# Linear attentions: the state's products before the level matrix's products in each result tile

## The chip, the cores and the metric

The kernel runs on one core of one Trainium2 chip. The metric is the device time of one execution in microseconds (us), lower is better. The core has a matrix engine (PE, with its weight loads listed apart as PEld), a vector engine (DVE), a scalar engine (ACT), GpSimd (POOL) and a sync engine (SP) that issues transfers. Matrix products land in PSUM; DVE and ACT read them from there.

## The reference

Two transformer blocks over 1024 tokens of width 1024. The change lies in the first one, which mixes two gated linear attentions (4 heads with values of 128, and 4 heads with values of 64; keys of 64 in both) with a stick-breaking attention. A linear attention of the reference, cut to what matters:

```python
def step(state, inp):                       # over chunks of the sequence
    q_c, k_c, v_c, g_c = inp
    b_cum = jnp.cumsum(g_c, axis=2)
    decay = jnp.exp(jnp.where(causal, b_cum[:, :, :, None, :] - b_cum[:, :, None, :, :], -jnp.inf))
    scores = jnp.einsum('bhtd,bhsd,bhtsd->bhts', q_c, k_c, decay)
    o_c = (jnp.einsum('bhts,bhsv->bhtv', scores, v_c)
           + jnp.einsum('bhtd,bhdv->bhtv', q_c * jnp.exp(b_cum), state))
    state = (jnp.exp(b_last)[..., None] * state
             + jnp.einsum('bhsd,bhsv->bhdv', k_c * jnp.exp(b_last - b_cum), v_c))
    return state, o_c
```

So a result is the sum of two products: the chunk's own scores with the values, and the decayed queries with the state carried in from the earlier chunks.

## The kernel before

The kernel takes chunks of 128 tokens, eight of them (`NT`), and treats the eight heads as four items of two heads each. Items 0 and 1 have values of 128 columns (`dv` 128), items 2 and 3 of 64. For an item:

- `gla_start` and `gla_state` make the carried state `S`, chunk by chunk: PE (L594) multiplies decayed keys and values into one PSUM tile `po` of which there is only one buffer, DVE (L599) adds it onto the decayed state before. These steps of the next item stand between the products of the present one.
- seven levels (`gla_level_a` to `gla_level_d`) fill the score matrices. For each, DVE takes differences (L619, L621), ACT exponentiates (L622), POOL and DVE multiply with keys and queries (L641, L643), PE makes eight products of 128 rows by 128 columns (L654) into a two-bank PSUM tile `gla_pb`, and DVE copies the cells of the level into `ST` (L663). `ST` holds the transposed score matrices of the whole item, 16 of 128 by 128, and exists once. Before the levels, DVE resets it with the diagonal (L606).
- `gla_qe` makes `qe`, the queries times the decay (ACT L667, DVE L668).
- `gla_out_a` makes the results. For each two-bank tile `po` of results (two for `dv` 128, one for `dv` 64) it issues, chunk by chunk and head by head, the product with `ST` (L686, it contracts over 128 rows) and for every chunk but the first the product with `S` (L688, it contracts over 64 rows). That is 16 and 14 products for an item, in either width. ACT then copies the tile out (L690).

All of these products are in fp32; the profile has two records for one. `gla_pb` and the result tiles `go_pb` share two PSUM buffers (`ps2`), so a result tile takes the buffer of the level before the last once that has been read.

Beside these steps, `fill` puts chunks of the block's input projections on PE (`unit_f`, L515 to L517, 128 by 512 moving columns, and `unit_v`) to use its time while the levels wait for other engines. They are used up before item 3 ends. After item 3 come its norm (`gla_out_b`, `gla_out_c`), the gate and the output projection of the block (L1124 to L1126), and then block two.

All engines run their own queue in order. The order in each queue is made when the program is built: the framework takes the instructions with their dependencies and lets a model of the timeline choose what comes next on each engine, so that an instruction written elsewhere can move others.

Of the kernel before, what the change touches and what calls it, by code (L numbers as in the profile page):

```python
# [15 lines left out]
P = 128  # L16
T = 1024
D = 1024
NT = T // P
# [135 lines left out]
class K:  # L155
# [516 lines left out]
    def gla_out_a(self, g):  # L672

        nc = self.nc
        S, v, dv, q, b, sc = (g[n] for n in ("S", "v", "dv", "q", "b", "sc"))
        st3 = self.ST.rearrange("p (c t) -> p c t", t=P)
        self.ph = f"go{dv}"
        qe = g["qe"] if "qe" in g else self.gla_qe(g, self.t4(tag="tmp"))
        g["o"] = []
        for i in range(2 * dv // P):  # L680
            po = self.ps2()
            for c in range(NT):
                cs = slice(c * P, (c + 1) * P)
                for h in ((i,) if dv == P else range(2)):
                    d = po[:, cs] if dv == P else po[64 * h:64 * h + 64, cs]
                    nc.tensor.matmul(d, v[:, c, h * dv:(h + 1) * dv], st3[:, 2 * c + h], start=True, stop=(c == 0))  # L686
                    if c:
                        nc.tensor.matmul(d, S[64 * h:64 * h + 64, c], qe[64 * h:64 * h + 64, cs], start=False, stop=True)  # L688
            o = self.gt("mx")
            nc.scalar.copy(o, po)  # L690
            g["o"].append(o)
# [1462 lines left out]
```

## Time and profile before

| | us |
|---|---|
| median of 3 runs (2403.15 to 2412.2) | 2404.36 |
| the profiled execution | 2410.1 |
| its span in the trace | 2408.2 |
| PE busy in it | 2255.4 (94%) |
| DVE busy | 1413.2 (59%) |
| POOL busy | 1169.6 (49%) |
| ACT busy | 892.4 (37%) |

The four places where results of an item are made lie at about 401 to 413, 489 to 511, 581 to 591 and 634 to 652 us of the span. The engines' shares over the whole span say little on these places, so they are read from the stretches around them. "PEclk" in a table of stretches is the granted clock of PE as a share of 2.4 GHz; 0.5 is its other level, 1.2 GHz. In the list of instructions in order of time, "x4" counts records (two for one fp32 product), the second number is the time from the first start to the last end, and what stands in square brackets is the idle time before and what ended it.

### The profile page before, as it was taken

Reading aid. Unit: us, or ns where it says so; the run is one execution under the profiler, and the core shown is the slowest. Engines: PE = TensorE matmul, PEld = TensorE weight load, DVE = VectorE, ACT = ScalarE, POOL = GpSimd, SP = SyncE. Lnnn points to the kernel's source line nnn. Section 1 sums busy time; section 2 is a strip of 40 time slices with the busy share of each in tenths; the row PEclk is TensorE's granted clock in tenths of the full one; section 3 lists DMA queues with packets and bytes.
Section 4 is the critical chain, followed back from the end, with each engine's and each line's share of the span. In section 5 each row is a group of like instructions: output and inputs, shape, how many; then the busy total and the mean of one; then the engine's idle time right before and its main releaser. Section 6 shows DMA issues by size and latency. Waiting matters only on the chain.

```text
span 2408.2 us, 30577 instructions
## 1 busy us (share of the span) xinstructions
PE 2255.4 (94%) x11689; PEld 1880.8 (78%) x11689; DVE 1413.2 (59%) x1982; ACT 892.4 (37%) x1459; POOL 1169.6 (49%) x924
## 2 busy tenths in 40 slices
PE   4999899999698999978999998999999999999997
PEld 3788787877577888767888886888888888888886
DVE  8576765758567457999867776436333333333335
ACT  4456632443214244855376775113211111111111
POOL 4247683654456353444467888520433443344331
PEclk9999989879599999989999999999999999999999
DMA  6442332312332222434531522331111111111112
GB/s 256 122 145 88 116 102 81 119 44 84 124 136 88 75 69 76 174 118 117 157 92 50 138 86 78 131 140 53 45 50 47 53 44 44 53 53 53 44 44 81
DMA packets 125759, 220.95 MB, mean 92 GB/s; under 512 B 48658, under 2 KB 72866, under 8 KB 125218
## 3 DMA queue, kind: packets, MB, share of 16 engines
q1 hardware_dynamic: 125602, 218.89, 27.4%
q8 instruction: 94, 1.54, 0.3%
q14 instruction: 63, 0.52, 0.1%
HBM read 166.85 MB, written 52.01 MB: 91 GB/s over the span
## 4 chain that ended last, share of the span: by engine, by line
PE 51%; DVE 5%; ACT 2%; issue 2%; POOL 1%; DMA 0%; POOLq 0%; DVEq 0%; ACTq 0%; SPq 0%
PE up_pb L1981 5%; PE up_pb L1979 5%; PE up_pb L1980 5%; PE br_ps L1925 3%; PE dn_ps L2034 3%; PE dn_ps L2036 3%; PE dn_ps L2035 3%; PE F_ps L230 2%; PE F_ps L228 2%; PE F_ps L229 2%; DVE topk_r L1589 2%; PE dn_pb L1980 1%; PE dn_pb L1981 1%; PE dn_pb L1979 1%; PE op_ps L1126 1%
## 5 line engine op out<-in xcount | busy, mean ns | idle before, releaser
L2038 DVE TENSOR_TENSOR br_h<-br_h,dn_ps 128x512 f32<-128x512 f32 x176 | 119.6, 685 | 237.6 <-PE dn_ps L2036 237.3
L205 POOL TENSOR_SCALAR up_wh<-up_raw 128x1024 fp32r<-128x1024 f32 x41 | 43.5, 1061 | 272.8 <-PE up_pb L1980 133.8
L2017 DVE SCALAR_TENSOR_TENSOR ffn_ws<-up_pb,cols,ffn_ws 128x1023 f32<-128x1023 f32 x66 | 84.5, 1281 | 138.9 <-ACT ffn_ws L2015 138.1
L2015 ACT ACTIVATE ffn_ws<-up_pb,cols 128x1024 f32<-128x1024 f32 x33 | 40.0, 1212 | 235.0 <-PE up_pb L1981 235.0
L1590 ACT ACTIVATE topk_r<-topk_r 128x896 bf16<-128x896 bf16 (+2 forms) x96 | 90.3, 945 | 58.8 <-DVE topk_r L1589 58.8
L210 POOL TENSOR_TENSOR up_wl<-up_raw,up_wh 128x1024 fp32r<-128x1024 f32 x41 | 98.5, 2403 | 20.2 <-PE up_pb L1981 17.5
L1979 PE MATMUL up_pb<-br_h,up_wh 128*128 128x512 f32 x264 | 102.7, 389 | 0.0
L1980 PE MATMUL up_pb<-br_h,up_wh 128*128 128x512 f32 x264 | 102.7, 389 | 0.0
L1981 PE MATMUL up_pb<-br_h,up_wl 128*128 128x512 f32 x264 | 102.7, 389 | 0.0
L1979 PE MATMUL up_pb<-op_fh,up_wh 128*128 128x512 f32 x264 | 102.7, 389 | 0.0
L1980 PE MATMUL up_pb<-op_fl,up_wh 128*128 128x512 f32 x264 | 102.7, 389 | 0.0
L1981 PE MATMUL up_pb<-op_fh,up_wl 128*128 128x512 f32 x264 | 102.7, 389 | 0.0
L2022 ACT CAST up_g<-ffn_ws 128x1024 fp32r<-128x1024 f32 x22 | 23.1, 1050 | 176.0 <-PE dn_ps L2035 97.7
L2034 PE MATMUL dn_ps<-dn_wh,up_g 128*128 128x512 f32 x192 | 75.2, 392 | 1.3 <-DVE br_h L2038 1.3
L242 PE MATMUL v_ps<-sb_wh,init_hh 128*128 128x256 f32 x256 | 75.1, 294 | 0.7 <-ACT v_st L500 0.7
L244 PE MATMUL v_ps<-sb_wh,init_hl 128*128 128x256 f32 x256 | 75.3, 294 | 0.0
L243 PE MATMUL v_ps<-sb_wl,init_hh 128*128 128x256 f32 x256 | 74.4, 291 | 0.7 <-POOL sb_wl L210 0.7
L2035 PE MATMUL dn_ps<-dn_wl,up_g 128*128 128x512 f32 x192 | 74.7, 389 | 0.0
L2036 PE MATMUL dn_ps<-dn_wh,up_g 128*128 128x512 f32 x192 | 74.7, 389 | 0.0
L210 POOL TENSOR_TENSOR sb_wl<-sb_raw,sb_wh 128x1024 fp32r<-128x1024 f32 x15 | 39.7, 2651 | 60.3 <-ACT sb_wh L209 41.7
L2020 POOL TENSOR_TENSOR ffn_ws<-ffn_ws 128x1024 f32<-128x1024 f32 x22 | 52.7, 2395 | 32.7 <-DVE ffn_ws L2017 32.7
L654 PE MATMUL gla_pb<-QB,gla_X 128*128 128x128 f32 x448 | 62.2, 291 | 6.5 <-POOL gla_X L643 6.5
(766 smaller groups left out, 7659.7 us busy)
## 6 DMA issues: line engine op xcount, KB each, us to landing
up_raw<-in_wu SPq DMA_DIRECT2D x43, 512.0 KB, 3.3
dn_raw<-in_wu SPq DMA_DIRECT2D x21, 512.0 KB, 3.2
sb_sp<-F_st SPq DMA_DIRECT2D x34, 256.0 KB, 2.0
sb_raw<-in_wu SPq DMA_DIRECT2D x15, 512.0 KB, 3.9
init_X<-in_wada SPq DMA_DIRECT2D x13, 512.0 KB, 4.3
c_raw<-in_wu SPq DMA_DIRECT2D x13, 512.0 KB, 3.4
br_raw<-in_wu SPq DMA_DIRECT2D x12, 512.0 KB, 3.8
bq_raw<-in_wu SPq DMA_DIRECT2D x11, 512.0 KB, 3.5
```

The source lines that it names most:

```text
L210: (nc.gpsimd if pool else nc.vector).tensor_tensor(l, raw, h, op=OP.subtract)
L242: nc.tensor.matmul(po, hh[:, k, ts], wh[:, cs], start=(k == 0), stop=False)
L244: nc.tensor.matmul(po, hl[:, k, ts], wh[:, cs], start=False, stop=(k == KT - 1))
L1590: nc.scalar.activation(y, y, AF.Copy, accum_out=cnt[:, j:j + 1])
L1979: nc.tensor.matmul(o, wh[:, s], self.hh[h][:, kk], start=(kk == 0), stop=False)
L1980: nc.tensor.matmul(o, wh[:, s], self.hl[h][:, kk], start=False, stop=False)
L1981: nc.tensor.matmul(o, wl[:, s], self.hh[h][:, kk], start=False, stop=(kk == KT - 1))
L2017: nc.vector.scalar_tensor_tensor(u[:, d:], p[:, :T - d], tap(2 - d), u[:, d:], op0=OP.mult, op1=OP.add)
L2034: nc.tensor.matmul(po, hi[:, ts], wh[:, cs], start=(k == 0), stop=False)
L2035: nc.tensor.matmul(po, hi[:, ts], wl[:, cs], start=False, stop=False)
L2036: nc.tensor.matmul(po, lo[:, ts], wh[:, cs], start=False, stop=(k == 1))
L2038: nc.vector.tensor_tensor(x, x, po, op=OP.add)
```

## The change

In each result tile, all products with `S` come first, head by head and chunk 1 to 7, and then all products with `ST`, chunk 0 to 7. The first product that is written into each of the two PSUM banks of a tile (chunk 1 and chunk 4) carries the start flag, and all the others accumulate. The number of products, their sizes and their operands are as before.

```diff
             po = self.ps2()
-            for c in range(NT):
-                cs = slice(c * P, (c + 1) * P)
-                for h in ((i,) if dv == P else range(2)):
-                    d = po[:, cs] if dv == P else po[64 * h:64 * h + 64, cs]
-                    nc.tensor.matmul(d, v[:, c, h * dv:(h + 1) * dv], st3[:, 2 * c + h], start=True, stop=(c == 0))
-                    if c:
-                        nc.tensor.matmul(d, S[64 * h:64 * h + 64, c], qe[64 * h:64 * h + 64, cs], start=False, stop=True)
+            heads = (i,) if dv == P else range(2)
+            d = lambda c, h: po[:, c * P:(c + 1) * P] if dv == P else po[64 * h:64 * h + 64, c * P:(c + 1) * P]
+
+            for h in heads:
+                for c in range(1, NT):
+                    nc.tensor.matmul(d(c, h), S[64 * h:64 * h + 64, c], qe[64 * h:64 * h + 64, c * P:(c + 1) * P],
+                                     start=c in (1, 4), stop=False, skip_group_check=True)
+            for h in heads:
+                for c in range(NT):
+                    nc.tensor.matmul(d(c, h), v[:, c, h * dv:(h + 1) * dv], st3[:, 2 * c + h], start=False, stop=True,
+                                     skip_group_check=True)
```

In the lists below, L687 and L691 of the changed kernel are L688 and L686 of the one before (products with `S`, products with `ST`), and later lines are shifted by four.

PE's queue at the results of item 1 (`go_pb_3998` is the first result tile, `gs_S` the state, `gs_po` the next item's state step, `F_ps` a projection), before:

```order
L517 MATMUL F_ps_4057<-init_hh_90,gla_wl_3918 128x512
L686 MATMUL go_pb_3998<-ST,gla_w_3123 128x128 [waits DVE_49]
L686 MATMUL go_pb_3998<-ST,gla_w_3123 128x128
L594 MATMUL gs_po_3840<-go_w_3592,gs_tmp_3818 64x64 [waits DVE_49]
L594 MATMUL gs_po_3840<-go_w_3592,gs_tmp_3818 64x64
L688 MATMUL go_pb_3998<-go_tmp_3995,gs_S_3253 128x128
L686 MATMUL go_pb_3998<-ST,gla_w_3123 128x128
L688 MATMUL go_pb_3998<-go_tmp_3995,gs_S_3253 128x128
```

The same place in the changed kernel:

```order
L516 MATMUL F_ps_4057<-init_hl_92,gla_wh_3917 128x512
L687 MATMUL go_pb_3998<-go_tmp_3995,gs_S_3253 128x128 [waits DVE_49]
L687 MATMUL go_pb_3998<-go_tmp_3995,gs_S_3253 128x128 x4
L594 MATMUL gs_po_3840<-go_w_3592,gs_tmp_3818 64x64 [waits DVE_49]
L594 MATMUL gs_po_3840<-go_w_3592,gs_tmp_3818 64x64
L687 MATMUL go_pb_3998<-go_tmp_3995,gs_S_3253 128x128 x2
L691 MATMUL go_pb_3998<-ST,gla_w_3123 128x128 x8
L687 MATMUL go_pb_4016<-go_tmp_3995,gs_S_3253 128x128
L594 MATMUL gs_po_3844<-go_w_3592,gs_tmp_3818 64x64 [waits DVE_49]
L594 MATMUL gs_po_3844<-go_w_3592,gs_tmp_3818 64x64
L687 MATMUL go_pb_4016<-go_tmp_3995,gs_S_3253 128x128 x6
L691 MATMUL go_pb_4016<-ST,gla_w_3123 128x128 x5
```

The alternation of the two sizes is gone. The set also begins four projection products earlier in the queue: nine of `F_ps_4057` stood ahead of it, now five do, and the four others stand behind it. The next item's state step still splits the sets.

DVE's queue before that place (`go_tmp_3995` is `qe`, and L663 is the last copy into `ST`), before:

```order
L668 TENSOR_TENSOR go_tmp_3995<-go_tmp_3995,gla_qkb_3117 128x1024 [waits Activation_49]
L745 SCALAR_TENSOR_TENSOR F_tmp_3888<-mix_mx_3893,F_tmp_3888 128x1024 [waits DMAHW5_49,DVE_49]
L619 TENSOR_TENSOR gla_X_4047<-go_qkb_3590 128x32x16
L621 TENSOR_TENSOR gla_X_4047<-go_qkb_3590 128x32x16
L663 COPY_PREDICATED ST<-lv,gla_pb_3950 128x1024 [waits PE_49]
L641 TENSOR_TENSOR QB_483<-gla_X_3962,go_qkb_3587 64x8x64 [waits Activation_49]
L599 SCALAR_TENSOR_TENSOR gs_S_3831<-gs_S_3831,gs_c_3766,gs_po_3836 128x64 [waits PE_49]
```

And in the changed kernel:

```order
L749 SCALAR_TENSOR_TENSOR F_tmp_3888<-mix_mx_3893,F_tmp_3888 128x1024 [waits DMAHW5_49,DVE_49]
L619 TENSOR_TENSOR gla_X_4047<-go_qkb_3590 128x32x16
L621 TENSOR_TENSOR gla_X_4047<-go_qkb_3590 128x32x16
L668 TENSOR_TENSOR go_tmp_3995<-go_tmp_3995,gla_qkb_3117 128x1024 [waits Activation_49]
L663 COPY_PREDICATED ST<-lv,gla_pb_3950 128x1024 [waits PE_49]
L641 TENSOR_TENSOR QB_483<-gla_X_3962,go_qkb_3587 64x8x64
L599 SCALAR_TENSOR_TENSOR gs_S_3831<-gs_S_3831,gs_c_3766,gs_po_3836 128x64 [waits PE_49]
```

The step that makes `qe` has moved back by three and now stands right ahead of the last copy into `ST`.

PE's queue at the results of item 3, where no projection is left (`gla_pb_4785` is the last level, `go_qkb_4664` is `qe`), before:

```order
L654 MATMUL gla_pb_4785<-QB_483,gla_X_4768 128x128 x7
L686 MATMUL go_pb_4800<-ST,go_w_3592 64x128 [waits DVE_49]
L686 MATMUL go_pb_4800<-ST,go_w_3592 64x128 x2
L688 MATMUL go_pb_4800<-go_qkb_4664,gs_S_4377 64x128
L686 MATMUL go_pb_4800<-ST,go_w_3592 64x128
L688 MATMUL go_pb_4800<-go_qkb_4664,gs_S_4377 64x128
```

And in the changed kernel:

```order
L654 MATMUL gla_pb_4785<-QB_483,gla_X_4768 128x128 x7
L687 MATMUL go_pb_4800<-go_qkb_4664,gs_S_4377 64x128 [waits DVE_49]
L687 MATMUL go_pb_4800<-go_qkb_4664,gs_S_4377 64x128 x13
L691 MATMUL go_pb_4800<-ST,go_w_3592 64x128 [waits DVE_49]
L691 MATMUL go_pb_4800<-ST,go_w_3592 64x128 x15
L708 MATMUL go_pg_4833<-h_488,go_tmp_4836 128x2 [waits PE_49,Activation_49]
```

Here there are two waits for DVE where there was one: 14 products behind the first, 16 behind the second.

## Rows read from the trace of the kernel before

**Rows 1.** Stretches: busy us (instructions) by engine, PE clock, DMA share, GB/s.

```profile
400.00:413.50 13.50, 13.50 (x73) 9.65 (x72) 1.12 (x3) 3.12 (x5) 1.26 (x1) 1.00 0.06 21
413.50:489.00 75.50, 72.08 (x397) 61.81 (x397) 58.32 (x52) 32.16 (x36) 46.70 (x22) 0.91 0.34 119
489.00:511.00 22.00, 21.56 (x74) 15.22 (x75) 5.87 (x9) 3.92 (x5) 4.25 (x3) 0.55 0.03 13
511.00:580.00 69.00, 65.67 (x377) 56.34 (x377) 58.54 (x57) 29.65 (x35) 36.28 (x19) 0.92 0.23 84
580.00:592.00 12.00, 12.00 (x78) 7.00 (x77) 2.89 (x4) 2.58 (x4) 1.26 (x1) 1.00 0.06 22
592.00:634.00 42.00, 26.88 (x188) 24.35 (x187) 40.54 (x31) 16.82 (x25) 30.87 (x20) 0.76 0.34 120
634.00:652.00 18.00, 17.52 (x60) 8.45 (x60) 1.72 (x3) 0.00 (x0) 0.56 (x1) 0.50 0.00 0
```

**Rows 2.** Who waited, 310 to 665 us: us in total, times, longest.

```profile
DVE ST L606 <- PE go_pb L686: 7.6, 3, 3.8
```

**Rows 3.** Item 0, PE in order of time: start us, us, records (x).

```profile
400.63 0.60 PE L686 MATMUL go_pb<-ST,sb_w 128*128 128x128 f32 x4
401.17 0.49 PE L688 MATMUL go_pb<-go_tmp,gs_S 64*128 64x128 f32 x2
401.58 0.49 PE L686 MATMUL go_pb<-ST,sb_w 128*128 128x128 f32 x2
...
413.38 0.49 PE L654 MATMUL gla_pb<-QB,gla_X 128*128 128x128 f32 x2
413.80 0.44 PE L594 MATMUL gs_po<-gla_w,gs_tmp 128*64 128x128 f32 x4
414.17 1.83 PE L654 MATMUL gla_pb<-QB,gla_X 128*128 128x128 f32 x14
```

**Rows 4.** Item 1, PE in order of time.

```profile
489.12 0.71 PE L686 MATMUL go_pb<-ST,gla_w 128*128 128x128 f32 x4 [1.74 <-DVE ST L663]
490.15 0.34 PE L594 MATMUL gs_po<-go_w,gs_tmp 128*64 128x64 f32 x4 [0.32 <-DVE gs_S L599]
...
491.25 0.79 PE L688 MATMUL go_pb<-go_tmp,gs_S 64*128 64x128 f32 x2
491.97 0.79 PE L686 MATMUL go_pb<-ST,gla_w 128*128 128x128 f32 x2
...
510.58 1.65 PE L654 MATMUL gla_pb<-QB,gla_X 128*128 128x128 f32 x6
```

**Rows 5.** Item 1, DVE in order of time: the last copy into ST.

```profile
486.62 2.44 DVE L663 COPY_PREDICATED ST<-lv,gla_pb 128x1024 f32<-128x1024 uint8 x1
```

**Rows 6.** Item 2, PE in order of time.

```profile
580.72 0.65 PE L686 MATMUL go_pb<-ST,go_w 128*64 128x128 f32 x6
...
591.27 2.05 PE L654 MATMUL gla_pb<-QB,gla_X 128*128 128x128 f32 x16
593.08 0.48 PE L515 MATMUL F_ps<-init_hh,gs_wh 128*128 128x512 f32 x1
```

**Rows 7.** Item 3 and what follows, all engines in order of time.

```profile
614.92 6.38 DVE L739 SCALAR_TENSOR_TENSOR go_tmp<-go_tmp,mix_X 128x1024 f32<-128x1024 f32 x1
...
615.14 3.78 PE L654 MATMUL gla_pb<-QB,gla_X 128*128 128x128 f32 x16 [6.47 <-POOL gla_X L643]
...
627.19 2.44 DVE L663 COPY_PREDICATED ST<-lv,gla_pb 128x1024 f32<-128x1024 uint8 x1
...
631.97 2.46 DVE L663 COPY_PREDICATED ST<-lv,gla_pb 128x1024 f32<-128x1024 uint8 x1
...
634.48 1.12 PE L686 MATMUL go_pb<-ST,go_w 128*64 128x128 f32 x6 [5.55 <-DVE ST L663]
...
652.28 1.01 ACT L690 COPY go_mx<-go_pb 128x1024 f32<-128x1024 f32 x1 [19.06 <-PE go_pb L688]
...
663.00 1.22 PE L1124 MATMUL op_ps<-mix_wh,F_mh 128*128 128x512 f32 x2
```

## Prediction

> **What bounds the kernel now.** PE is busy for most of the span, but that says nothing about a place of 10 to 20 us, so I read the table of stretches first [rows 1]. At the results of items 0, 1 and 2 (13.5, 22 and 12 us) PE is busy throughout, while DVE has 1.12, 5.87 and 2.89 us of work: the other engines wait for these products. In the two long stretches between, PE is busy for 72.08 of 75.5 and 65.67 of 69 us, and DVE for 58.32 and 58.54. PE is the bound there too, with DVE 10 to 17 us behind. Between 592 and 634 us it turns round: DVE 40.54 of 42 us, PE 26.88. The last stretch, 634 to 652 us, holds PE's products for item 3 and next to nothing else.
>
> The list of who waited gives the link from one item to the next: DVE's reset of `ST` waits for the last product that reads it, 7.6 us over three items [rows 2]. So an earlier end of the products with `ST` starts the next item's levels earlier.
>
> Then PE's list in order of time, place by place. In item 0 products of the two sizes alternate and start 0.41 to 0.42 us apart [rows 3]; eight level products of one size take 593.08 - 591.27 = 1.81 us, 0.226 each [rows 6]. A change of size therefore costs about 0.19 us at 2.4 GHz. Check: the item's 30 products with 28 changes and two state steps of 0.37 us (414.17 - 413.80) make 30 x 0.226 + 28 x 0.19 + 0.74 = 12.8 us, and 413.38 - 400.63 = 12.75 us is what they took [rows 3]. That PSUM accumulation in place causes the gap is excluded by the same rows: the state step L594 between two level products adds to neither tile, and the pair from 413.38 to 414.17 costs 0.79 us, 0.56 more than one product. In item 1 the spacing becomes 491.97 - 491.25 = 0.72 us [rows 4], with the granted clock at 0.55 over the stretch [rows 1], that is 1.2 GHz for most of it; PE had stood idle for 1.74 and 0.32 us just before. Eight products of one size at that level span 3.78 us [rows 7], about 0.45 each, so a change costs about 0.27 there.
>
> **The change, part by part.** It adds and removes no product. It takes away most changes of size, lets the products with `S` start before `ST` is ready, and moves a few neighbours.
>
> *Item 0.* By the new order, seven with `S`, state step, eight with `ST`, four, state step, three, eight. A state step between products of one size costs 0.56 [rows 3], one between two sizes 0.37 and a change. Sum: 30 x 0.226 + 3 changes x 0.19 + 0.56 + 0.56 = 8.5 us, 4.3 less.
>
> *Item 1.* `qe` now ends right before the last copy into `ST`, so the first five products with `S` (1.1 us) lie beside that copy, 486.62 to 489.06 [rows 5]. Nothing is gained yet: the state step behind them waits for DVE's L599, which still follows the copy, and starts at 490.15 as before [rows 4]. Behind that wait stand the 25 other products and the next levels. From 490.15 at full clock: step 0.27, 25 x 0.226, 4 changes, two steps of 0.56 inside a size, together 7.8 us, and four projection products (about 0.9 us) that before stood ahead: 498.9 where the trace has 510.58, 11.7 less. At 1.2 GHz from 491.25 on, as in the trace, 21 to 22 products at 0.45, 3 changes at 0.27, steps of 0.8 and projections of 1.8 end at about 505.2, 5.4 less. I take 8.5, the middle, since the idle time that went ahead of the low clock is still there, while the products behind it are closer together. The Trainium skill ("TensorE: Matmul & The Clock Gate", Part 1) says that "the default state is throttled, and activity releases the throttle". By that rule the denser set would regain 2.4 GHz inside the place, and the term would lie towards 11.7; the trace has the low level through the sparse set and cannot show the dense one.
>
> *Item 2.* 591.27 - 580.72 = 10.55 us [rows 6] become 30 x 0.226 plus three changes and two steps, about 7.9: 2.6 less. The price of a change in this width, from the same rows, is (10.55 - 6.8 - 0.6) / 28 = 0.11.
>
> *Item 3.* The result tile takes the buffer that DVE's copy from 627.19 to 629.63 reads [rows 7]. After it the 14 products with `S` can run in PE's idle 5.55 us ahead of 634.48: 14 x 0.226 = 3.2 us, at the low clock 6.3. They end between 632.8 and 635.9. The 16 with `ST` still wait for the last copy (634.43) and take 3.6 to 7.2 us. ACT's copy, at 652.28 before, starts between 638.1 and 642; with the products with `S` not begun early it would be 634.5 + 30 x 0.45 = 648. So 4 to 14 less; I take 11.3, near the low clock that this stretch shows (0.50) for the second set. What is late next is the same chain as before, the norm and the gate, which leads to the output projection at 663.00 without PE work beside it, so all of this term shifts the rest.
>
> *The other moves* (a `qe` step on DVE, state steps, two gate steps and their loads near 610 us) I cost at nothing: the same instructions, beside PE's work in the first three stretches. Where that cover is gone, near 615 us, L739 took 6.38 us [rows 7]; its start may move by a few us in either direction. I keep +-5 us for it.
>
> *Price of a product with 64 rows behind another with 64 rows.* No row shows it. Nearest rows: 0.226 (128 rows behind 128) and 0.41 (64 behind 128). It cannot cost more than with a change ahead of it, nor much less than a product that streams the same 128 columns. I take 0.226, as the stream is the same and only the rows in use differ. A rule of the Trainium skill speaks against it: "TensorE: Matmul & The Clock Gate", Part 3, What overlaps and what doesn't, has weight loads run beside products only where the row group differs. By it each product with `S` would go on paying its load, and the whole gain would be the second rival's below. In rows 6 eight level products in the same rows run at 0.226 with a load each, against that rule; for 64 rows no run here shows it.
>
> *Sum.* Items 0 to 2: 4.3 + 8.5 + 2.6 = 15.4, of which I let 14 through, since DVE has less than 17 us in hand in the stretches behind them and the state step still comes one at a time. With item 3: 14 + 11.3 = 25 us. The profiled execution (2410.1, its span 2408.2 and 1.9 around it) would take 2385; it lies 5.7 above the median of 2404.36, from which the forecast is 2379.
>
> **The rivals.**
>
> *Only the tail gains.* If DVE and POOL set the pace of the levels, what items 0 to 2 give is waited away. For: DVE is at 77 and 85% in the long stretches. Against: PE at 95% in the same rows, and DVE's waits for it. Then item 3 alone, 11.3: 2393.
>
> *Products with 64 rows stay slow* (0.41 each, 0.72 at the low clock). Half the changes' price stays: about 2 + 4.5 + 1 in items 0 to 2, and in item 3 the first set lasts until 638 to 640 and the second until 645, 7 less. Together about 14: 2390.
>
> *The clock turns it slower.* PE is done sooner and then waits for DVE and POOL; each wait can bring the low clock, as before 491 us. Its place is the two long stretches, where the projections run: a product that takes 0.226 takes 0.45, so each us of PE time at 1.2 GHz costs half a us. Their clock is 0.91 and 0.92 [rows 1], some 12 to 14 and 11 us at the low level. To eat 25 us it would take 50 more of their 145 us, a mean clock near 0.75, and it decides beyond that; at 0.65 (77 us more, 38 lost) the kernel would be 13 us slower: 2417. Against: after the results PE has projections to do at once, and only 3.4 us idle in each stretch now.
>
> *It doesn't do what it says*: DVE's waits could be set by a later instruction so that the first set waits for the last copy after all. In items 0 and 2 that changes nothing, in item 3 it gives 648: a total of about 18, 2386, inside the forecast's range.
>
> **How the numbers follow.** The forecast 0.70, only the tail 0.13, slow products 0.10, the clock 0.04, more than 36 us gained 0.03. The forecast's own range: items 0 to 2 between 11 and 19, item 3 between 4 and 14, the moved steps +-5, added without all ends at once: 15 to 35 us, 2369 to 2389. The two rivals at 2390 and 2393 are taken in, so 2368 to 2394 for 8 times in 10. Half a per cent is 12 us, about what a measurement of this kernel tells from no change. The forecast is wholly beyond it, the 14 of the slow products mostly, the 11 of the tail alone nearly half: 0.70 + 0.03 + 0.06 + 0.05 makes 0.84 for faster; slower 0.04; no change 0.12.
>
> **What would show it.** In the profile after: products with `S` and with `ST` 0.226 us apart inside a set (0.45 at the low clock); item 0's place 8 to 9 us long; item 1's first five products with `S` beside DVE's last copy and the state step behind them waiting; in item 3 the 14 products ahead of the copy's end and ACT's copy some 4 us after the copy into `ST` (full clock) or 7 (low). The output projection should start 25 us earlier than 663, and everything behind it be as before. Wrong would be: 0.4 us inside a set of 64 rows; a mean clock under 0.85 in the stretches between; or places that are shorter with an output projection that isn't 15 us earlier.

## The result and the profile after

The changed kernel takes 2368.20 us (median of 4, 2364.39 to 2375.75), the kernel before 2405.51 beside it: a ratio of 0.9842 [0.9816, 0.9869], about 37 us less. A second set of runs gave 2370.9 against 2408.56, 0.9844 [0.9814, 0.9874]. The forecast was 25 us less; the direction and the mechanism held, the size was half as large again. On the earlier median of 2404.36 the ratio gives 2366.4, just below 2368, the low end of the range.

The stretches of the changed kernel (columns as in [rows 1]), cut at the same places of the program:

```profile
396.50:406.00 9.50, 9.50 (x76) 8.15 (x76) 0.94 (x3) 3.38 (x5) 1.26 (x1) 1.00 0.08 29
406.00:476.00 70.00, 68.14 (x395) 58.56 (x396) 57.40 (x52) 32.02 (x37) 43.28 (x21) 0.95 0.38 128
476.00:488.00 12.00, 10.56 (x77) 9.36 (x77) 4.66 (x9) 3.93 (x5) 6.89 (x4) 0.86 0.06 23
488.00:554.00 66.00, 63.03 (x369) 54.35 (x368) 57.08 (x52) 29.68 (x34) 37.82 (x19) 0.95 0.24 88
554.00:563.00 9.00, 8.47 (x78) 7.26 (x78) 5.29 (x9) 2.29 (x4) 2.30 (x2) 1.00 0.27 90
563.00:598.00 35.00, 24.71 (x188) 22.46 (x187) 31.81 (x30) 15.84 (x23) 22.75 (x16) 0.85 0.35 129
598.00:606.00 8.00, 7.24 (x70) 6.63 (x69) 7.21 (x5) 1.43 (x3) 7.83 (x5) 1.00 0.00 0
```

All four places of results are shorter, and PE's clock at items 1 and 3 is 0.86 and 1.00 where it was 0.55 and 0.50. The stretches between are shorter too, with the clock at 0.95, 0.95 and 0.85 where it was 0.91, 0.92 and 0.76.

PE in order of time at items 0, 1 and 2, which answers to [rows 3, 4, 6]:

```profile
397.25 1.83 PE L687 MATMUL go_pb<-go_tmp,gs_S 64*128 64x128 f32 x14
399.00 0.44 PE L594 MATMUL gs_po<-gla_w,gs_tmp 128*64 128x128 f32 x4
399.37 2.05 PE L691 MATMUL go_pb<-ST,sb_w 128*128 128x128 f32 x16
...
475.50 1.38 PE L687 MATMUL go_pb<-go_tmp,gs_S 64*128 64x128 f32 x10
478.31 0.34 PE L594 MATMUL gs_po<-go_w,gs_tmp 128*64 128x64 f32 x4 [1.44 <-DVE gs_S L599]
478.58 0.71 PE L687 MATMUL go_pb<-go_tmp,gs_S 64*128 64x128 f32 x4
479.22 3.27 PE L691 MATMUL go_pb<-ST,gla_w 128*128 128x128 f32 x16
...
483.43 1.60 PE L687 MATMUL go_pb<-go_tmp,gs_S 64*128 64x128 f32 x12
484.96 1.38 PE L691 MATMUL go_pb<-ST,gla_w 128*128 128x128 f32 x10
...
487.31 1.95 PE L654 MATMUL gla_pb<-QB,gla_X 128*128 128x128 f32 x16
...
555.51 1.30 PE L687 MATMUL go_pb<-go_tmp,gs_S 64*64 64x128 f32 x10
557.34 0.34 PE L594 MATMUL gs_po<-go_w,gs_tmp 128*64 128x64 f32 x4 [0.53 <-DVE gs_S L599]
...
562.66 1.61 PE L654 MATMUL gla_pb<-QB,gla_X 128*128 128x128 f32 x12
```

Seven products with `S` (14 records) start within 1.75 us, 0.25 each with the change to the state step; a 64-row product behind another does not pay for a change of size. At item 1 the first set lies beside the last copy into `ST`, and the state step behind it still waits for DVE (1.44 us), as forecast. The eight products behind 479.22 take 3.27 us, a mix of the two clock levels, and from 483.43 on six take 1.60 us again: the clock came back inside the place.

That copy in DVE's list, which answers to [rows 5]:

```profile
474.79 2.45 DVE L663 COPY_PREDICATED ST<-lv,gla_pb 128x1024 f32<-128x1024 uint8 x1
```

And the line on DVE's reset of `ST` among those who waited (us, times, longest), which answers to [rows 2]:

```profile
DVE ST L606 <- PE go_pb L691: 4.6, 3, 2.5
```

The reset waits 3.0 us less than before, since the last product that reads `ST` ends sooner.

All engines at the end of the levels, item 3 and behind, which answers to [rows 7]:

```profile
592.79 1.22 DVE L743 SCALAR_TENSOR_TENSOR gla_qkb<-gla_qkb,mix_X 128x1024 f32<-128x1024 f32 x1
592.89 5.93 POOL L766 TENSOR_TENSOR F_ml<-mix_tmp,F_mh 128x512 fp32r<-128x512 f32 x4 [2.99 <-ACT F_mh L764]
...
599.02 2.89 PE L687 MATMUL go_pb<-go_qkb,gs_S 64*64 64x128 f32 x28
599.84 2.45 DVE L663 COPY_PREDICATED ST<-lv,gla_pb 128x1024 f32<-128x1024 uint8 x1
...
602.34 3.33 PE L691 MATMUL go_pb<-ST,go_w 128*64 128x128 f32 x32 [0.43 <-DVE ST L663]
...
605.71 1.01 ACT L694 COPY go_mx<-go_pb 128x1024 f32<-128x1024 f32 x1 [4.63 <-PE go_pb L691]
...
615.01 1.22 PE L1128 MATMUL op_ps<-mix_wh,F_mh 128*128 128x512 f32 x2
```

The 14 products with `S` lie beside the last copy, the 16 with `ST` follow it at 2.4 GHz, and ACT's copy starts 3.4 us after the copy into `ST` ended (17.9 before). The gate step L743 takes 1.22 us, beside POOL's subtractions (L766), where L739 took 3.26 and 6.38. The output projection starts 48.0 us earlier.

These 48.0 us are more than the medians differ, because the profiled execution of before lies above its median and the first one of after below its own. So the account below uses the profile of the second set, whose time is its median (2370.9, span 2369.0). "Place" is first start to last end of an item's result products; in brackets the us of it at 1.2 GHz, summed from the trace's clock records.

| us | before | after, second set | less | forecast |
|---|---|---|---|---|
| up to item 0 | 400.63 | 400.06 | 0.6 | 0 |
| item 0 | 12.82 (0) | 8.47 (0) | 4.4 | 4.3 |
| stretch to item 1, and item 1 | 75.7 (13.7) + 21.5 (19.4) | 72.2 (13.7) + 13.4 (6.8) | 11.5 | 8.5 |
| stretch to item 2, and item 2 | 70.1 (11.3) + 10.6 (0) | 68.0 (6.8) + 7.3 (0) | 5.5 | 2.6 |
| end of item 2 to the end of the last copy into `ST` | 43.1 | 39.6 | 3.5 | 0 |
| that copy to the last product | 17.8 (17.8) | 3.4 (0) | 14.4 | 11.3 |
| all behind it | 1756.0 | 1756.7 | -0.7 | 0 |
| sum | 2408.2 | 2369.0 | 39.2 | 26.7, of which 25 let through |

### The profile page after: what moved, and what is told of

Its sections match the earlier page's. It is cut to its first block, busy times and chain, and to the rows that moved or that the text cites. A ratio compares the mean times of both kernels' runs of the same rounds, so it can differ in the third digit from the quotient of the medians.

```text
span 2362.5 us, 30584 instructions
## 1 busy us (share of the span) xinstructions
PE 2212.0 (94%) x11689; PEld 1859.5 (79%) x11689; DVE 1412.4 (60%) x1982; ACT 892.0 (38%) x1459; POOL 1170.1 (50%) x924
## 4 chain that ended last, share of the span: by engine, by line
PE 52%; DVE 5%; ACT 2%; issue 2%; POOL 1%; DMA 0%; POOLq 0%; DVEq 0%; ACTq 0%; SPq 0%
PE up_pb L1983 5%; PE up_pb L1984 5%; PE up_pb L1985 5%; PE br_ps L1929 3%; PE dn_ps L2038 3%; PE dn_ps L2040 3%; PE dn_ps L2039 3%; PE F_ps L230 2%; PE F_ps L228 2%; PE F_ps L229 2%; DVE topk_r L1593 2%; PE dn_pb L1985 1%; PE dn_pb L1984 1%; PE dn_pb L1983 1%; PE attB_ps L217 1%
## 5 line engine op out<-in xcount | busy, mean ns | idle before, releaser
L2038 PE MATMUL dn_ps<-dn_wh,up_g 128*128 128x512 f32 x192 | 75.2, 392 | 1.3 <-DVE br_h L2042 1.3
L210 POOL TENSOR_TENSOR sb_wl<-sb_raw,sb_wh 128x1024 fp32r<-128x1024 f32 x15 | 40.0, 2673 | 59.7 <-ACT sb_wh L209 41.4
L654 PE MATMUL gla_pb<-QB,gla_X 128*128 128x128 f32 x448 | 59.8, 285 | 10.3 <-DVE QB L641 10.3
L2024 POOL TENSOR_TENSOR ffn_ws<-ffn_ws 128x1024 f32<-128x1024 f32 x22 | 52.7, 2394 | 32.7 <-DVE ffn_ws L2021 32.7
```

Source lines behind the costliest of these rows:

```text
L210: (nc.gpsimd if pool else nc.vector).tensor_tensor(l, raw, h, op=OP.subtract)
L2038: nc.tensor.matmul(po, hi[:, ts], wh[:, cs], start=(k == 0), stop=False)
```

## The experiments

The theory at the outset: the gain is the change of size that no longer happens, and it is larger than forecast because the denser sets run at 2.4 GHz at items 1 and 3. Rivals: the early start of the products with `S`; accumulation in place; the two parts acting on each other; the alternation itself lowering the clock.

### Grouped, but with `ST` first

```diff
             for h in heads:
+                for c in range(NT):
+                    nc.tensor.matmul(d(c, h), v[:, c, h * dv:(h + 1) * dv], st3[:, 2 * c + h], start=c in (0, 4),
+                                     stop=False, skip_group_check=True)
+            for h in heads:
                 for c in range(1, NT):
                     nc.tensor.matmul(d(c, h), S[64 * h:64 * h + 64, c], qe[64 * h:64 * h + 64, c * P:(c + 1) * P],
-                                     start=c in (1, 4), stop=False, skip_group_check=True)
-            for h in heads:
-                for c in range(NT):
...
+                                     start=False, stop=True, skip_group_check=True)
```

> The two sets of a tile stay whole, but the products with ST come first and those with S behind them, so nothing can start ahead of the last copy into ST. Theory (the gain is the removed changes of size, at the clock level of the place; I took the low level in items 1 and 3 where the denser sets got the full one): items 0 to 2 as in the changed kernel, each product 0.226 us from the next; item 3 needs all 30 products after the copy, 6.5 us at 2.4 GHz or 13 at 1.2, where the changed kernel needs 3.4. So 27 to 35 us faster than before, ratio 0.985 to 0.989. Rival (the early start makes most of it: products with S beside DVE's copies, which also keep the clock up): the gain falls by half or more, 20 us or less, ratio 0.9915 or above.

Measured: 2381.07 us, ratio 0.9892 [0.9875, 0.9908], about 26 us less, just short of the 27 to 35 expected. Items 0 to 2 take 8.56, 11.67 and 6.89 us. At item 3, PE in order of time:

```profile
613.53 4.97 PE L687 MATMUL go_pb<-ST,go_w 128*64 128x128 f32 x32 [5.62 <-DVE ST L663]
618.43 2.89 PE L691 MATMUL go_pb<-go_qkb,gs_S 64*64 64x128 f32 x28
```

All 30 products now stand behind the copy, and PE is idle for 5.62 us ahead of them. The first 16 mix both levels, the last 14 are at 2.4 GHz. So grouping alone gives some 26 of the 37 us. Of the 11 that the order of the two sets adds, the profiles show 4.4 at item 3 (7.8 us behind the copy against 3.4) and 3.8 in the stretch ahead of it (43.4 us to the end of the copy against 39.6).

### The new order in item 3 alone, and in items 0 to 2 alone

```diff
+        self.nout = getattr(self, "nout", -1) + 1
...
+            if self.nout == 3:
+                heads = (i,) if dv == P else range(2)
...
+            else:
+                for c in range(NT):
+                    cs = slice(c * P, (c + 1) * P)
...
```

That is item 3 alone; for items 0 to 2 the condition is `!= 3`. The first branch is the changed kernel's code, the second that of before.

> The new order in item 3 alone, items 0 to 2 alternate as before. Theory: item 3 gives what it gives in the changed kernel, since its clock is decided by its own set: ACT's copy of the result 4 us after the last copy into ST instead of 18, 14 us, ratio 0.994. Rival (item 3 ran at the full clock only because the stretch before it came out denser): products 0.45 us apart, 10 us, ratio 0.996.

> The new order in items 0 to 2, item 3 alternates as before. Theory: items 0 to 2 give 4, 12 to 13 and 3 to 6 us and the stretches between let them through, 18 to 25 us, ratio 0.990 to 0.9925; item 3 stays at 11 to 18 us. Rival (only the tail gains, what is won at items 0 to 2 is waited away): 0 to 8 us, ratio 0.997 or above.

Measured: item 3 alone 2392.38 us, 0.9941 [0.9924, 0.9958], 14 us less; items 0 to 2 alone 2387.49 us, 0.9923 [0.9894, 0.9953], 18.5 us less. Together 32.7, against 37: within the intervals the two parts add, and what the early items give is not waited away (the rival "only the tail gains" is false).

Item 1 of the kernel that changes item 3 alone has the same products in the same order as before. PE in order of time there:

```profile
484.23 0.71 PE L700 MATMUL go_pb<-ST,gla_w 128*128 128x128 f32 x4 [1.75 <-DVE ST L663]
485.27 0.34 PE L594 MATMUL gs_po<-go_w,gs_tmp 128*64 128x64 f32 x4 [0.32 <-DVE gs_S L599]
485.53 0.48 PE L702 MATMUL go_pb<-go_tmp,gs_S 64*128 64x128 f32 x2
485.95 0.49 PE L700 MATMUL go_pb<-ST,gla_w 128*128 128x128 f32 x2
```

The idle times ahead are those of [rows 4], 1.75 and 0.32 us, and yet the spacing stays at 0.42 us to the end of the place: 13.37 us with none at 1.2 GHz, where before had 21.53 with 19.4. The level at this place differs between executions of one order. What the trace of before showed there was one of two cases, not the price of the order.

Item 3 of that kernel did not give quite what it gives in the changed kernel:

```profile
616.15 2.89 PE L689 MATMUL go_pb<-go_qkb,gs_S 64*64 64x128 f32 x28 [0.92 <-DVE ST L663]
620.96 4.82 PE L693 MATMUL go_pb<-ST,go_w 128*64 128x128 f32 x32 [1.92 <-DVE ST L663]
```

The set with `S` ends early there, PE stands idle for 1.92 us ahead of the set with `ST`, and the first 3.1 us of that set are at 1.2 GHz: 4.9 us from the end of the copy to the last product, against 3.4. So the set alone does not decide its level, as the theory had it; what PE does just before it counts too.

In the other kernel, with the new order at item 1 and the clock full throughout, it is 7.45 us from the state step to the next levels, where the prediction had 7.8 for full clock:

```profile
483.68 0.34 PE L594 MATMUL gs_po<-go_w,gs_tmp 128*64 128x64 f32 x4 [1.56 <-DVE gs_S L599]
...
491.13 1.95 PE L654 MATMUL gla_pb<-QB,gla_X 128*128 128x128 f32 x16
```

### The order of before with products of one size

```diff
-                        nc.tensor.matmul(d, S[64 * h:64 * h + 64, c], qe[64 * h:64 * h + 64, cs], start=False, stop=True)
+                        nc.tensor.matmul(d, S[:, c], qe[:, cs], start=False, stop=True)
```

The products with `S` contract over all 128 rows, so each adds the other head's part as well; the order is that of before, and nothing starts early.

> The order of before, products alternate and accumulate in place, but the products with S use all 128 rows of S and of the queries (both heads together, so the results differ from the reference's). Number, columns and operands' tiles are as before; only the change of size is gone. Theory: a product every 0.21 to 0.23 us in items 0 to 2, item 0 in 8 to 9 us instead of 12.75; 25 to 33 us faster, ratio 0.986 to 0.990. Rival (the gap comes from accumulating in place right behind the first write, or from switching operands): spacing stays at 0.4 us and the time within 0.3% of before.

Measured: 2366.78 us, 0.9834 [0.9817, 0.9851], as much as the change itself and more than the 25 to 33 us expected. Item 0, PE in order of time:

```profile
395.32 0.39 PE L688 MATMUL go_pb<-go_tmp,gs_S 128*128 128x128 f32 x2
395.54 0.39 PE L686 MATMUL go_pb<-ST,sb_w 128*128 128x128 f32 x2
```

The two kinds still alternate and still accumulate in place, and stand 0.22 us apart instead of 0.42. So, in the width of 128, the change of size is the whole price, and accumulation in place has none. The places are 7.99, 9.06, 3.88 and 5.37 us. In the width of 64 the two heads write different halves of the result's rows, and their products overlap here, since each head's neighbour is the other one. The changed kernel, which goes head by head, doesn't have that gain, so the equal totals are partly chance.

### Both heads side by side

Two versions of the new order. The first takes the heads inside the chunks, in both sets; the second does so and also opens both result tiles of items 0 and 1 at once, so that the products with `S` come from the upper and the lower 64 rows in turn.

```diff
-            for h in heads:
-                for c in range(1, NT):
+            for c in range(1, NT):
+                for h in heads:
...
```

> The changed kernel with the two loops of each set exchanged: chunk by chunk, both heads. It differs for dv 64 alone, where two heads use different columns of the array (and for the products with S different rows). Theory (products of different parts of the array run beside each other, as the pairs of the kernel before do that start 0.007 us apart): the set of 16 with ST takes 1.8 us instead of 3.4 in items 2 and 3, the set of 14 with S 1.6 instead of 2.9; on the path are item 2's two sets and item 3's second, 3 to 5 us faster than the changed kernel, ratio to before 0.982 to 0.984. Rival (the copy into ST or the state step decides, not PE): no difference to the changed kernel within 0.1%.

> As with the heads in pairs, and for dv 128 both result tiles are opened and their products with S alternate between the two halves of the rows, into different banks; then the products with ST of the first tile, then of the second. Theory: 14 products with S take half of their 3 us in items 0 and 1, one change of size less in each; 3 us faster than with the heads in pairs in item 0, less in item 1, where they stand beside the copy. Rival: ACT's copy of the first tile now comes later and both PSUM buffers are held for longer, the next item's first level waits: 0 to 3 us slower than with the heads in pairs.

Measured: 2368.04 us, 0.9839 [0.9814, 0.9863], and 2366.36 us, 0.9831 [0.9806, 0.9855], beside 2370.9 for the changed kernel on the same chip. PE at item 3 of the first:

```profile
598.85 1.75 PE L687 MATMUL go_pb<-go_qkb,gs_S 64*64 64x128 f32 x28
601.97 1.97 PE L691 MATMUL go_pb<-ST,go_w 128*64 128x128 f32 x32 [1.38 <-DVE ST L663]
```

And at item 0 of the second:

```profile
398.09 1.16 PE L685 MATMUL go_pb<-go_tmp,gs_S 64*128 64x128 f32 x14
```

28 records in 1.75 us instead of 2.89, 32 in 1.97 instead of 3.33, and 14 in 1.16 instead of 1.83: products in different halves of the array do run beside each other. The places become 8.47, 10.80, 6.14, 5.09 and 6.94, 10.83, 4.43, 5.29 us. Of the 3 us expected from the second at item 0, 1.5 came. But 4.5 us over the whole is within what these runs can tell, and part of it lies beside the copy into `ST` at item 3. The second version has the lowest median of these; that it beats the changed kernel is not shown.

### Products thrown away ahead of the old order

To see whether the alternation or what stands ahead of it sets the clock: the order of before, with products that the first one with a start flag overwrites, ahead of items 1 and 3. First with the 64-row products themselves (7 and 21), then with 128 by 128 products of the identity (8 and 16).

```diff
+            for r in range((0, 8, 0, 16)[self.nout] if i == 0 else 0):
+                c = r % NT
+                nc.tensor.matmul(po[:, c * P:(c + 1) * P], self.ident, self.ident, start=True, stop=True)
```

> The order of before, plus products that are thrown away: ahead of the results of item 1 seven products with S, ahead of item 3 twenty-one, written into the result tile and overwritten. Their number roughly fills PE's idle time there. They change no size inside the sets. Theory (the low clock at items 1 and 3 came from the idle time ahead, and it was the price of it that I mis-sized): item 1's alternation runs at 0.41 us instead of 0.72 and item 3's at 0.36 instead of 0.6, 8 + 7 us faster, ratio 0.993 to 0.995. Rival (the low clock comes from the alternation itself, which leaves the array idle between products): no difference, or slower by the added 28 products, 1.000 to 1.003.

Measured: 2411.58 us, 1.0016 [1.0001, 1.0031]: the theory as written failed, and the places are 26.46 and 26.91 us, thrown-away products included. At item 3:

```profile
621.89 2.05 PE L654 MATMUL gla_pb<-QB,gla_X 128*128 128x128 f32 x16
626.29 9.22 PE L686 MATMUL go_pb<-go_qkb,gs_S 64*64 64x128 f32 x42 [2.35 <-DVE ST L663]
635.44 1.11 PE L693 MATMUL go_pb<-ST,go_w 128*64 128x128 f32 x6
```

PE was at full clock at 621.89 and then idle for 2.35 us; 21 products of 64 rows by 64 columns, with no gap between them, then took 9.22 us, 0.44 each, all at 1.2 GHz, and so did everything behind them. These products did not bring the clock back.

> The order of before, with 8 thrown-away products of the identity (128 rows, 128 columns, dense) ahead of item 1's results and 16 ahead of item 3's; each fills time in which PE stood idle (1.74 and 5.55 us) and is overwritten by the first product with start. Their results enter nothing. Theory: alternation keeps the clock level with which it begins, and dense products over 128 rows and 128 columns bring 2.4 GHz back where 64-row ones did not. Then item 1's place should take some 13.4 us instead of 21.5 (as the same instructions did in the kernel with the new order in item 3 alone) and item 3's some 10.8 instead of 17.8: 8 + 7 us less, 2 us of that given back for throw-away products that overrun the idle time, ratio 0.993 to 0.996. Rival: the alternation itself lowers the clock whatever stands ahead of it; then the places stay near 21 and 18 us and the ratio is 1.000 to 1.002.

Measured: 2403.53 us, 0.9983 [0.9970, 0.9997], right at one place and wrong at the other:

```profile
480.58 1.72 PE L685 MATMUL go_pb<-idr 128*128 128x128 f32 x14
485.54 0.48 PE L594 MATMUL gs_po<-go_w,gs_tmp 128*64 128x64 f32 x4 [3.23 <-DVE gs_S L599]
...
487.53 0.79 PE L692 MATMUL go_pb<-go_tmp,gs_S 64*128 64x128 f32 x2
...
629.10 3.84 PE L685 MATMUL go_pb<-idr 128*128 128x128 f32 x32 [0.47 <-DVE ST L663]
633.92 0.65 PE L690 MATMUL go_pb<-ST,go_w 128*64 128x128 f32 x6 [0.98 <-DVE ST L663]
634.51 0.43 PE L692 MATMUL go_pb<-go_qkb,gs_S 64*64 64x128 f32 x2
```

At item 3 the filled time ends with PE at full clock, and the alternating set behind it runs from 633.92 to 644.32: 10.40 us with none at 1.2 GHz, close to the 10.8 that was expected, and 7.4 less than the 17.77 of the same set before. So of the 14.4 us that the change gains there, about half is the clock and half the order, the early start of the products with `S` included. At item 1 PE had done the filling products early and then stood idle for 3.23 us at the state step; the alternating set behind it ran at 1.2 GHz (0.72 us apart) and gave back part of what item 3 won. The rival as put, whatever stands ahead, is false: behind the fillers of item 3 the alternation ran through at 2.4 GHz, as it does at item 0 of before. But a start at 2.4 GHz does not secure the level: at item 1 of before the place begins at 2.4 GHz, with 1.74 and 0.32 us of idle time at its start [rows 4], and falls 2.1 us on, inside the set. In none of the traces did a set that alternates the two sizes get back from 1.2 GHz.

### The gate steps' term by itself

The traces taken so far fall into two classes by the time from item 2's last product to the end of the last copy into `ST`: 43.1 to 43.4 us in before, with item 3 alone, with `ST` first, with 128 rows and with the thrown-away products of the identity; 39.6 in the changed kernel (both sets), with items 0 to 2 alone and with both pairings, and 39.3 with the thrown-away 64-row products. In the first class both of DVE's gate steps (L739 of before) are long, 6.38 and 3.26 us, or, with `ST` first, one of them (3.26) and two other steps (5.53 and 3.83). In the second both take 1.22 or 1.23, and with the thrown-away 64-row products 1.25 and 2.18. Test: the order of before, with the four subtractions that POOL does beside these steps put on DVE.

```diff
-            eng = nc.gpsimd if j in (1, 2, 3, 7) else nc.vector
+            eng = nc.gpsimd if j in (1, 2) else nc.vector
```

> The order of before, with the last four subtractions of the split (L762, 128 by 512, those that POOL does in 5.91 us beside DVE's gate step L739 near 615 us) on DVE. Theory: L739 lasted 6.38 and 3.26 us because POOL's steps ran beside it, and the changed kernel gained 3.5 us of this stretch because its gate steps fell elsewhere (1.23 and 1.22 us there). Then L739 should take 1.2 to 1.3 us both times, DVE gets 4 x 0.69 = 2.8 us more, and from item 2's last result to the end of the last copy into ST there are 38 to 41 us where there were 43.1: 2 to 5 us less, ratio 0.998 to 0.999. Rival: L739 is long for another reason (its input, its own wait); then it stays at 6 us, the stretch becomes 43 to 46 us and the ratio 1.000 to 1.002.

Measured: 2407.2 us, 1.0005 [0.9988, 1.0023], no difference. DVE in order of time:

```profile
613.36 1.24 DVE L739 SCALAR_TENSOR_TENSOR go_tmp<-go_tmp,mix_X 128x1024 f32<-128x1024 f32 x1
...
616.74 4.16 DVE L762 TENSOR_TENSOR F_ml<-mix_tmp,F_mh 128x512 fp32r<-128x512 f32 x2
620.83 2.05 DVE L739 SCALAR_TENSOR_TENSOR gla_qkb<-gla_qkb,mix_X 128x1024 f32<-128x1024 f32 x1
```

With POOL's subtractions moved, the first step went from 6.38 to 1.24 us and the second from 3.26 to 2.05. But the moved subtractions are long in their turn (4.16 us for two, 1.28 for the other two) beside POOL's next work, and the stretch is 41.4 us: 1.6 less instead of 2 to 5.

That such a step is long whenever it lies beside POOL's subtractions is not so. With the thrown-away 64-row products (L746 and L769 there are L739 and L762) it lies beside the same four:

```profile
617.53 1.25 DVE L746 SCALAR_TENSOR_TENSOR go_tmp<-go_tmp,mix_X 128x1024 f32<-128x1024 f32 x1
617.66 7.36 POOL L769 TENSOR_TENSOR F_ml<-mix_tmp,F_mh 128x512 fp32r<-128x512 f32 x4
```

Here DVE's step is short and POOL's four take 7.36 us, where they took 5.91 beside the 6.38. So beside each other one of the two is long, and which one differs from trace to trace. The Trainium skill ("Trainium Architecture — The Big Picture", What this means for kernel authors) has DVE and GpSimd contend for a shared port pair, as an exclusive lock; the traces agree as far as one of the two is long in each of these cases. This run has the order of before and yet 39.3 us, so the 3.5 us go with which engine is held up and not with the order of PE's products. What decides that was not tested by itself.

## Why the prediction was right in kind and short in size

The step that failed is the clock: the prediction carried the low level of the trace of before into item 3's last set and into the stretch behind item 1. The changed kernel ran that set at 2.4 GHz and had 4.5 us less at 1.2 GHz in that stretch, which gave 3.1 and 2.1 us more than forecast. To this come moves that it put at nothing, 3.5 and 1.5 us.

- **Item 0**, 4.3 forecast, 4.4 measured: right, as was the price of a change (0.19 us): the kernel with 128 rows has 0.22 us where there were 0.42.
- **Price of a 64-row product behind another**: taken as 0.226; the rows give 0.21 (item 3) to 0.26 (item 0). The rival "products with 64 rows stay slow" is false. The rule weighed there (the Trainium skill, "TensorE: Matmul & The Clock Gate", Part 3) does not hold here: products in the same rows, with a load each, do not pay for the loads.
- **Item 1**, 8.5 forecast, 11.5 measured with the stretch ahead. The prediction took the middle between full clock (11.7) and the low one (5.4), "since the idle time that went ahead of the low clock is still there". That stood for 510.58 - 8.5 - 490.15 = 11.9 us from the state step to the next levels, some 1.4 of them for the four projection products. In the traces these stand behind the next levels' first products, so 10.5 is what to compare. The second set takes 494.02 - 483.72 = 10.3, with 6.8 of the place at 1.2 GHz; the first profile 487.31 - 478.31 = 9.0, with 3.4; the new order in items 0 to 2 alone 7.45, with none. So the middle fits one execution and is too long for the others. Where the clock fell, it came back inside the place, just behind the set with `ST`. The prediction weighed this by the rule that activity releases the low clock (the Trainium skill, "TensorE: Matmul & The Clock Gate", Part 1) and did not follow it far enough; the trace agrees with the rule at this set, and does not at the 21 thrown-away products of 64 by 64. The other 1.5 us lie ahead of the place: the state step comes 75.2 us behind item 0 where it came 76.7, though by the prediction "nothing is gained yet". Why, no run shows.

```profile
483.72 0.48 PE L594 MATMUL gs_po<-go_w,gs_tmp 128*64 128x64 f32 x4 [1.57 <-DVE gs_S L599]
...
494.02 1.95 PE L654 MATMUL gla_pb<-QB,gla_X 128*128 128x128 f32 x16
```

- **Item 2**, 2.6 forecast, 3.4 measured at the place itself; 2.1 more us in the stretch ahead, which had 11.3 us at 1.2 GHz before and 6.8 after. In before the low clock of item 1 lasted 4.5 us beyond its place; in the changed kernel it ended inside.
- **Item 3**, 11.3 forecast, 14.4 measured: the failed step at its plainest, "near the low clock that this stretch shows". That 1.2 GHz came with PE's 5.55 us without work [rows 7]: with products of the identity in that time the old order ran at 2.4 GHz throughout. In the changed kernel the products with `S` fill it, and PE goes into the last set at full clock in both traces. The prediction's own sum for full clock was 14.2.
- **The other moves**, taken at 0 with +-5: the stretch gave 3.5, where DVE's gate steps took 1.23 and 1.22 us instead of 6.38 and 3.26. The bound held it; the value taken did not. Since the old order shows 39.3 us there too, this part is luck of the queues, not the forecast's mechanism.
- **What is let through**: 15.4 was cut to 14. No cut is to be seen: by the table what items 0 to 2 gave is still there at the last copy into `ST`, and the two parts tried alone add up to the whole within their intervals.

With 3.0 + 2.9 + 3.5 + 3.1 from these steps, and with the 1.7 between the sum of 26.7 and the rounded 25, the 25 become 39, the difference of the two profiled spans. The range lost at its low end because items 0 to 2 gave 21.4 us where its end was 19, and item 3 14.4 where it was 14, while the terms were added "without all ends at once". The clock of the trace of before lay under both, so one assumption put both off the same way. The rival in which the clock turns it slower did not come: in none of the stretches between the items did the changed kernel spend more time at 1.2 GHz than before.

What stays open: how much of the clock's rise in the stretches is due to the change. From 280 us to item 0, where little differs, before had 13.7 us at 1.2 GHz, the two profiles of after 3.4 and 10.2, and the kernels with the old order there between 6.8 and 13.7, so several us vary between executions whatever the kernel. What stands behind item 3's last product, the same in all, takes 1754.5 to 1763.3 us in the twelve traces, with 50 to 77 us of it at 1.2 GHz; a difference of a few us over the whole is not to be read from one profile.

## What to carry to other kernels

Count the changes of a product's size in PE's queue: here each cost 0.11 to 0.27 us in which nothing is gained, and grouping the sizes or giving all products one size removed it. Where a place runs at 1.2 GHz, work out both levels and ask whether the changed order removes what went ahead of the fall; terms that are taken from the same level of one trace share that assumption, and the range must let them go together. A step whose duration differs between two traces of the same instruction is worth a look at what the neighbouring engine did.

## What the runs showed of the hardware

- A change between 128 and 64 rows of contraction in successive fp32 products costs 0.19 us at 2.4 GHz where the result has 128 rows (0.42 us apart against 0.22 with one size, though these accumulate in place as well).
- A set that alternates the two sizes ran for 10.40, 12.82 and 13.37 us wholly at 2.4 GHz and for 17.77 us wholly at 1.2. It can fall inside, as at item 1 of before, but none got back. 21 gapless products of 64 by 64 stayed at 1.2 GHz for 9.22 us as well, while the places with the sizes grouped got back to 2.4 inside (3.4 and 6.8 us at 1.2 at item 1).
- Products in different halves of the array ran beside each other when neighbours in the queue: 28 records in 1.75 us against 2.89.
- Beside each other, a DVE step of 128 by 1024 and POOL's four subtractions took 6.38 and 5.91 us in one trace, 1.25 and 7.36 in another. With the four off POOL the step took 1.24.
